# A diffusion step: other queues for the u and y transfers, and GELU in fused operations with its second half behind the first splits of the GLU

## The chip, the cores and the metric

The kernel runs on one core of one Trainium2 chip. The metric is the device time of an execution, in microseconds. Three runs of the kernel before took 2743.68, 2744.83 and 2745.60 us, so the median is 2744.83.

## The reference, cut to what matters

One layer runs over 640 tokens, 128 of context and 512 latent ones, of width 2048. An adaLN-modulated, normalised input goes through one projection into `u_a`, `v_a` and `u_b`, of 1024 columns each. A chunk mixer takes the first two, a bidirectional state-space mixer the third; both are normalised and projected by `w_out`; a squared-ReLU MLP follows. The change lies in the state-space mixer:

```
u = x.reshape(bsz, seq_len, N_SSM_GROUPS, SSM_GROUP)          # 64 groups of 16
h_f = ssm_scan(u, lam_f, bb_f, h0_f, False)
h_b = ssm_scan(u, lam_b, bb_b, h0_b, True)
y = (einsum("ghp,blgp->blgh", c_f, h_f) + einsum("ghp,blgp->blgh", c_b, h_b)).real
y = y.reshape(bsz, seq_len, D_SSM) + d_skip * x
y = gelu(y)                                                   # tanh form
y = y * sigmoid(y @ w_glu + b_glu)
```

All is float32. Large products are made of three products of float32r halves, so each weight chunk is split into a high part (`wh`, ScalarE) and a low part (`wl`, VectorE), and so is each activation.

## The kernel before, in words

**Layout.** Tokens stand in 80 blocks of L=8 and one empty column, NJ=81 in all. The projection gives `u` with channels on partitions; the scan wants (time in block, channel of group) on partitions. So `u` goes through DRAM (`ud`): for each of 8 channel blocks `cb` a tile `us` is filled by VectorE (L324) and stored by 8 DMAs, one for each time in the block (L327). Odd ones are issued by ScalarE, even ones by GpSimd. Each moves 128 rows of 81 floats. The tile `us` has two buffers.

**The slots.** From L442 on the instructions of each engine are kept in the order in which the code issues them (`P`, `Kept`; the profile gives all of them one line, L451, so they are told apart by tiles). Work is cut into slots (`slot`, L496). A slot asks for the raw weights of chunk c+2 on SP (`raw_of`), makes the high part of chunk c+1 on ScalarE (`hi_of`) and the low part on VectorE (`lo_of`), and multiplies chunk c on TensorE. Other work is put into a slot by `at(t, phase, f)`: `sp`, `evac`, `act`, `dve`, `pe`, `end` in that order, and `mid0` and `mid1` within an `as` chunk.

**The stretch of the change.** Slots 33 to 48 multiply the chunk mixer's half by `w_out` (tiles `as`, 30 matmuls of 512 columns a slot). When the scan is done, which is at slot e = 42 here, `s5_rest` spreads 16 pieces `s5_out(u)` over the slots from e on, three a slot. Each makes 12 small products into a PSUM tile `yp` (two buffers), and ScalarE copies it over the input tile `U`. After u = 7 (slot 44) half 0 of y is complete, after u = 15 (slot 47) half 1. `y_store(half)` writes a half to DRAM (`yd`) with 8 DMAs, four on SP and four on ScalarE, each 16 partitions by 32 rows of 81 floats. `yc_load(k)` reads 128 channels back, blocks 0 to 3 from half 0 and 4 to 7 from half 1, and waits for all stores of its half. `gelu(k)` computes tanh-GELU into `yb`. `yb_split(k)` makes the two halves of `yb` that the GLU multiplies. The first two GLU chunks (`glu_pair`) take two column blocks: the first chunk needs blocks k = 0 to 3, the second k = 4 to 7.

**Before**, half 0 is stored in slot 45 and loaded in 46 and 47; gelu 0 and 1 stand in slot 47, 2 and 3 in 48; half 1 is stored at the end of 47, loaded in 48, and gelu 4 to 7 stand at the end of 48. Slot 49 splits blocks 0 to 3, multiplies the first GLU chunk, and splits 4 to 7.

[...]

Of the kernel before, what the change touches and what calls it, by code (L numbers as in the profile page):

```python
# [12 lines left out]
F32 = mybir.dt.float32  # L13
# [3 lines left out]
AF = mybir.ActivationFunctionType  # L17
OP = mybir.AluOpType
# [5 lines left out]
NT = 640  # L24
# [3 lines left out]
GH = 16  # L28
NS = 64
L = 8  # L30
NJ = 81
# [12 lines left out]
def build(nc, tc, a, out, tap=None):  # L44
    tap = tap or {}
    V = nc.vector
    S = nc.scalar
    G = nc.gpsimd
# [8 lines left out]
    def a20(shape, dt, name):  # L57
        return fr.tile(shape, dt, name=name, tag="a20", bufs=4)
# [4 lines left out]
    def pm(name="pm"):  # L63
        return pp.tile([128, 512], F32, name=name, tag="pm", bufs=4)
# [16 lines left out]
    def dram(name, shape):  # L81
        return dr.tile(shape, F32, name=name)
# [4 lines left out]
    yd = dram("yd", [DC, L, NJ])  # L87
# [79 lines left out]
    def load_w(src, n1, n2, prio=WPRIO):  # L167

        with tc.high_priority(offset=prio):
            raw = wtile("r", [128, n1, n2], F32)  # L170
            nc.sync.dma_start(raw, src)
            hi = wtile("h", [128, n1, n2], F32R)
            lo = wtile("l", [128, n1, n2], F32R)
            S.activation(hi, raw, AF.Copy)
            V.tensor_sub(lo, raw, hi.bitcast(F32))
        return hi, lo
# [5 lines left out]
    def ws_mm(ps, hi, lo, k, kk, c, ah, al, first, last, tr):  # L182
        for i, (st, mv) in enumerate(((hi, ah), (hi, al), (lo, ah))):
            for p, (t0, n) in zip(ps, tr):
                T.matmul(p[:, :n], st[:, kk, c:c + 128], mv(k)[:, t0:t0 + n],  # L185
                         start=(first and i == 0), stop=(last and i == 2))
# [39 lines left out]
    for tb in range(NTB):  # L226
        if tb:
            for n in range(2):
                p = pm("pos")
# [70 lines left out]
    def u_chunk(kc0, nk):  # L300
        kb = slice(kc0, kc0 + nk)
        cpl = 8 // nk
        for cb in range(8):
            if cb % cpl == 0:
                whi, wlo = load_w(w_in[:, kb, 2 * DC + cb * 128:2 * DC + (cb + cpl) * 128], nk, cpl * 128, 0)
            ps = [pm("ub"), pm("ub")]
            for k in range(kc0, kc0 + nk):
                ws_mm(ps, whi, wlo, k, k - kc0, (cb % cpl) * 128, ah, al, k == kc0, k == kc0 + nk - 1, FULL)
            if kc0 + nk == NK and cb == 6:
                ahead.append(load_w(w_in[:, 0:8, DC:DC + 128], 8, 128, 0))  # L310
            if kc0 + nk < NK:
                for p_, (t0, n) in zip(ps, FULL):
                    dst = uacc[:, cb, t0:t0 + n]
                    if kc0 == 0:
                        S.activation(dst, p_[:, :n], AF.Copy)
                    else:
                        V.tensor_add(dst, dst, p_[:, :n])
            else:
                us = main.tile([128, L, NJ], F32, name="us", tag="t25", bufs=2)
                V.memset(us[:, :, 16:17], 0.0)  # L320
                jt = lambda t: t.rearrange("p (j t) -> p t j", t=L)
                for i, t0, n, j0 in ((0, 0, 128, 0), (0, 128, 192, 17), (1, 320, 320, 41)):
                    o = t0 - i * 320
                    V.tensor_tensor(us[:, :, j0:j0 + n // L], jt(uacc[:, cb, t0:t0 + n]), jt(ps[i][:, o:o + n]), op=OP.add)  # L324

                for t in range(L):
                    (nc.scalar if t % 2 else nc.gpsimd).dma_start(  # L327
                        bass.AP(tensor=ud.tensor, offset=ud.offset + ((7 - t) * GH * NG + cb * 8) * NJ,
                                ap=[[NJ, 8], [NG * NJ, GH], [1, NJ]]), us[:, t, :])

    for i in range(len(CH) + 1):
        if i < len(CH):
            h_chunk(*CH[i])
        if i:
            u_chunk(*CH[i - 1])
# [44 lines left out]
    q, w = vt_[3], vt_[4]  # L380
# [19 lines left out]
    for lo_, n in ((1, 1), (2, 2), (4, 4)):  # L400
        for d in range(2):
# [8 lines left out]
            t2 = p0.tile([128, 4, NG], F32, name="pt", tag="acs", bufs=2)  # L410
# [42 lines left out]
    V, S, T, G, SY = [Kept(e) for e in (nc.vector, nc.scalar, nc.tensor, nc.gpsimd, nc.sync)]  # L453
# [5 lines left out]
    def at(t, phase, f):  # L459
        assert t >= now[0], (t, now[0], phase)  # L460
        todo.setdefault((t, phase), []).append(f)
# [334 lines left out]
    HG = 32  # L796
    JS = NJ + 1
    Us, pbs = [], {}
    ydv = yd.rearrange("(g c) t j -> t c g j", c=GH)
# [140 lines left out]
    for h in range(8):  # L940
        t = t0_ + 2 * h
# [74 lines left out]
    def s5_out(uu):  # L1016
        t_, o_ = so_.pop(uu)
        half, u = divmod(uu, 8)
        U = Us[half]
        p = px("yp")  # L1020
        for g in range(4):
            gg = u * 4 + g
            gx = half * HG + gg
            o = p[:, g * NJ:(g + 1) * NJ]
            T.matmul(o, t_[:, g, :], U[:, gg, :], start=True, stop=False)
            T.matmul(o, o_[:, 0, g, :], X[:, 0, gx, 0:NJ], start=False, stop=False)
            T.matmul(o, o_[:, 1, g, :], X[:, 1, gx, 1:1 + NJ], start=False, stop=True)
        S.activation(U[:, u * 4:u * 4 + 4, :], p[:, 0:4 * NJ].rearrange("p (g j) -> p g j", j=NJ), AF.Copy)
        so_load(uu + 3)

    def y_store(half):
        for tq in range(8):
            (SY if tq % 2 else S).dma_start(ydv[tq][:, half * HG:(half + 1) * HG, :], Us[half][tq * GH:(tq + 1) * GH])

    K0 = float(np.sqrt(2.0 / np.pi))
    yb, ycs = [None, None], {}
    ybs = []

    def yb_part(k, lo):
        return ybs[lo][:, k, :]  # L1040

    ybk = lambda k: yb[k // 4][:, k % 4, :]

    def yc_load(k):
        if k < 4:
            ycs[k] = main.tile([128, L, NJ], F32, name="yc", tag="t25", bufs=2)
        else:
            if k % 2 == 0:
                ykeep.append(pbs["pb"].tile([128, 1536], F32, name="yk", tag="so", bufs=3))
            ycs[k] = ykeep[-1][:, k % 2 * 768:k % 2 * 768 + L * NJ].rearrange("p (t j) -> p t j", t=L)  # L1050
        SY.dma_start(ycs[k], yd[k * 128:(k + 1) * 128])

    def gelu(k):
        yc = ycs.pop(k)
        if k % 4 == 0:
            yb[k // 4] = pbs["uy"].tile([128, 4, NT], F32, name="yb", tag="uy", bufs=2)
        w1 = pbs["pb"].tile([128, L, NJ], F32, name="w1", tag=("ya", "vc")[k % 2], bufs=1)
        S.activation(w1, yc, AF.Square)
        V.tensor_scalar(w1, w1, 0.044715, 1.0, op0=OP.mult, op1=OP.add)
        V.tensor_mul(w1, w1, yc)  # L1060
        S.activation(w1, w1, AF.Tanh, scale=K0)
        V.tensor_scalar(w1, w1, 1.0, 0.5, op0=OP.add, op1=OP.mult)
        for c0, c1, j0 in ((0, 128, 0), (128, 640, 17)):
            nj = (c1 - c0) // L
            V.tensor_tensor(ybk(k)[:, c0:c1].rearrange("p (j t) -> p t j", t=L), w1[:, :, j0:j0 + nj],
                            yc[:, :, j0:j0 + nj], op=OP.mult)

    def yb_split(k):
        if k == 0:
            ybs.extend(a20([128, 8, NT], F32R, f"yb{i}") for i in range(2))  # L1070
        S.activation(yb_part(k, 0), ybk(k), AF.Copy)
        V.tensor_sub(yb_part(k, 1), ybk(k), yb_part(k, 0).bitcast(F32))
# [41 lines left out]
    def s5_rest(e):  # L1114

        where = [(e + u // 3, (("mid0", "mid1", "pe") if e + u // 3 < 49 else ("pe",) * 3)[u % 3]) for u in range(16)]
        for u, w in enumerate(where):
            at(*w, lambda u=u: s5_out(u))
        t, t2 = where[7][0], where[15][0]
        at(t + 1, "sp", lambda: y_store(0))  # L1120
        for k in range(4):
            at(t + 2 + k // 2, "sp", lambda k=k: yc_load(k))
            at(t + 3 + k // 2, "act", lambda k=k: gelu(k))
        at(t2, "end", lambda: y_store(1))
        for k in range(4, 8):
            at(t2 + 1, "sp", lambda k=k: yc_load(k))
            at(t2 + 1, "end", lambda k=k: gelu(k))
        return t + 5, t2 + 1

    flow[0] = iter(())  # L1130
    e = None
    t = 16
    while t < 49 or e is None or t < max(g0, g1):
# [4 lines left out]
        if scanned and e is None and t >= 38:  # L1138
            e = t
            g0, g1 = s5_rest(e)  # L1140
# [14 lines left out]
    g1 = max(g1, g0)  # L1155
    for k in range(4):
        at(g0, "act", lambda k=k: yb_split(k))
        at(g1, "end", lambda k=4 + k: yb_split(k))
    t = g0
    while cur[0] < len(chunks):  # L1160
        c = cur[0] - 48
# [18 lines left out]
    V, S, T, G = nc.vector, nc.scalar, nc.tensor, nc.gpsimd  # L1180
# [146 lines left out]
    half = lambda w: w.rearrange("(j t p) c -> t p j c", t=2, p=128)  # L1327
# [347 lines left out]
    p = ps["2"].tile([128, 512], F32, name="trms", tag="zp", bufs=2)  # L1675
# [83 lines left out]
```

## Time and profile before

| | |
|---|---|
| median of three runs | 2744.83 us |
| profiled execution | 2745.85 us |
| its span | 2744.0 us, 43078 instructions |
| TensorE (PE) | 2608.5 us busy, 95% |
| VectorE (DVE) | 1939.3 us, 71% |
| ScalarE (ACT) | 1116.6 us, 41% |
| GpSimd (POOL) | 85.3 us, 3% |
| DMA | 519.37 MB, mean 189 GB/s |

PE is TensorE's matmuls, PEld its weight loads, SPq and ACTq the instructions with which SP and ScalarE issue DMAs; those of GpSimd stand under POOL. Busy time of TensorE is 95% of the span, so the other engines' shares say little by themselves. What matters is the few places where TensorE stands still, and which instruction ended that.

### The profile page before, as it was taken

What the parts mean: (1) busy time and instruction counts of PE and PEld (TensorE: products, weight loads), DVE (VectorE), ACT (ScalarE), POOL (GpSimd) and SP (SyncE); (2) the same over time, 40 slices, a digit from 0 to 9 for tenths busy, and PEclk for the clock granted to TensorE, in tenths of its full rate; (3) what the DMA queues carried; (4) which work ended last, traced back from release to release, by engine and by line L of the source; (5) the groups of instructions that cost most, each with busy time, mean ns of one, the idle gap of its engine ahead of it and who ended that gap; (6) DMA issues with size and microseconds to landing.
All of it is one profiled execution on the core that took longest, in us unless ns stands there. A gap on an engine that the chain in (4) does not pass through costs nothing.

```text
span 2744.0 us, 43078 instructions
## 1 busy us (share of the span) xinstructions
PE 2608.5 (95%) x17217; PEld 2410.7 (88%) x17217; DVE 1939.3 (71%) x2870; ACT 1116.6 (41%) x1806; POOL 85.3 (3%) x105
## 2 busy tenths in 40 slices
PE   8997999989959988899999999998999999999997
PEld 5687888877848665899999999998999999999996
DVE  4565997888055356777777777776677777777786
ACT  4121432222134255655555555554433232323253
POOL 0003221000001000000000000000000000000000
PEclk9998999999979998899999999999999999999998
DMA  9846766454746796355665556557466356446553
GB/s 302 293 165 158 213 199 204 143 182 151 202 103 222 253 334 204 89 177 176 186 183 173 178 174 188 181 176 267 132 219 219 114 196 219 158 148 227 179 174 112
DMA packets 459434, 519.37 MB, mean 189 GB/s; under 512 B 31409, under 2 KB 375633, under 8 KB 451809
## 3 DMA queue, kind: packets, MB, share of 16 engines
q1 hardware_dynamic: 440240, 507.84, 56.9%
q10 hardware_dynamic: 17456, 7.43, 1.1%
q8 instruction: 136, 2.23, 0.3%
q0 software_dynamic: 1536, 1.35, 0.2%
q14 instruction: 66, 0.53, 0.1%
HBM read 410.08 MB, written 106.45 MB: 188 GB/s over the span
## 4 chain that ended last, share of the span: by engine, by line
PE 82%; DMA 6%; DVE 6%; ACT 3%; issue 2%; SPq 1%; POOL 0%; ACTq 0%; DVEq 0%; POOLq 0%
PE X L1381 32%; PE Y L1381 16%; PE Z L1381 8%; PE ws L451 7%; PE ub L185 4%; PE ob L1284 3%; PE as L451 3%; PE ada L195 2%; DMA vc<-vd 2%; PE adaq L451 1%; PE yp L451 1%; DMA x2d<-wx 1%; DMA wr<-in_w_out_dram 1%; PE adaq L195 1%; PE x1p L451 1%
## 5 line engine op out<-in xcount | busy, mean ns | idle before, releaser
L1368 ACT ACTIVATE wh<-wx 128x1024 fp32r<-128x1024 f32 x223 | 235.8, 1058 | 310.1 <-PE X L1381 140.8
L1373 DVE TENSOR_TENSOR wl<-wx,wh 128x1024 fp32r<-128x1024 f32 x223 | 272.8, 1223 | 73.9 <-ACT wh L1368 71.9
L1381 PE MATMUL X<-B,wh 128*128 128x320 f32 x1376 | 308.0, 312 | 3.3 <-ACT wx L1368 3.3
L1381 PEld LDWEIGHTS X<-B,wh 128*128 128x128 f32 x1376 | 233.7, 191 | 3.6 <-ACT wx L1368 3.6
L1381 PE MATMUL X<-B,wl 128*128 128x320 f32 x688 | 214.2, 311 | 0.0
L1381 PE MATMUL X<-B,wx 128*128 128x320 f32 x1008 | 154.6, 309 | 0.0
L1381 PE MATMUL Y<-B,wh 128*128 128x320 f32 x672 | 150.6, 312 | 3.5 <-ACT wh L1368 3.5
L1381 PEld LDWEIGHTS X<-B,wx 128*128 128x128 f32 x1008 | 149.5, 188 | 0.0
L1456 DVE TENSOR_TENSOR wx<-wx 128x320 fp32r<-128x320 f32 x192 | 93.0, 485 | 78.2 <-ACT wx L1453 78.2
L1579 DVE TENSOR_TENSOR facc<-facc,X 128x640 f32<-128x640 f32 x116 | 95.1, 820 | 73.1 <-PE X L1381 72.4
L451 ACT ACTIVATE wh<-wr 128x1024 fp32r<-128x1024 f32 x55 | 58.3, 1060 | 207.7 <-DMA wr<-in_w_in_dram 82.1
L1381 PE MATMUL X<-B2n,wh 128*128 128x320 f32 x608 | 134.7, 309 | 0.0
L1381 PEld LDWEIGHTS X<-B,wl 128*128 128x128 f32 x688 | 131.0, 190 | 0.0
L451 DVE TENSOR_TENSOR wl<-wr,wh 128x1024 fp32r<-128x1024 f32 x55 | 68.5, 1246 | 84.9 <-ACT wh L451 84.3
L1368 ACT ACTIVATE wh<-wr 128x1024 fp32r<-128x1024 f32 x76 | 80.4, 1058 | 107.5 <-PE X L1381 51.3
L451 PE MATMUL ws<-hTh,wh 128*128 128x320 f32 x512 | 122.6, 321 | 0.4 <-DVE us L324 0.4
L451 PE MATMUL ws<-hTh,wl 128*128 128x320 f32 x512 | 118.9, 314 | 3.6 <-DVE wl L451 3.6
L1368 ACT ACTIVATE wx<-wr 128x1024 fp32r<-128x1024 f32 x75 | 79.4, 1058 | 104.7 <-PE X L1381 53.3
L1368 ACT ACTIVATE wx<-wx 128x1024 fp32r<-128x1024 f32 x74 | 78.3, 1058 | 103.5 <-PE X L1381 48.7
L451 PE MATMUL ws<-hTl,wh 128*128 128x320 f32 x512 | 118.7, 313 | 0.0
L1381 PEld LDWEIGHTS Y<-B,wh 128*128 128x128 f32 x672 | 113.9, 190 | 3.8 <-ACT wh L1368 3.8
L1373 DVE TENSOR_TENSOR wx<-wr,wx 128x1024 fp32r<-128x1024 f32 x75 | 91.8, 1224 | 28.0 <-ACT wx L1368 27.3
(380 smaller groups left out, 6685.5 us busy)
## 6 DMA issues: line engine op xcount, KB each, us to landing
wx<-in_w_ff_dram SPq DMA_DIRECT2D x169, 512.0 KB
x2d<-wx SPq DMA_DIRECT2D x224, 320.0 KB
wr<-in_w_ff_dram SPq DMA_DIRECT2D x87, 512.0 KB
aw<-in_w_ada_dram SPq DMA_DIRECT2D x80, 512.0 KB
was<-in_w_ada_dram SPq DMA_DIRECT2D x64, 512.0 KB
B2n<-x2d SPq DMA_DIRECT2D x24, 1280.0 KB
wr<-in_w_in_dram SPq DMA_DIRECT2D x48, 512.0 KB
wr<-in_w_out_dram SPq DMA_DIRECT2D x48, 512.0 KB
```

The lines of the kernel that those rows point to most:

```text
L185: T.matmul(p[:, :n], st[:, kk, c:c + 128], mv(k)[:, t0:t0 + n], start=(first and i == 0), stop=(last and i == 2))
L195: T.matmul(p[32 * j:32 * j + 32], sc[:, 2 * (k0 + i):2 * (k0 + i) + 32], w[:, i, :], start=k0 + i < 4, stop=k0 + i >= NK - 4)
L451: return lambda *p, **k: P(f(*p, **k))
L1284: T.matmul(p, st[:, k0 + kk, tsl], mv[:, kk, :], start=(k0 + kk == 0 and i == 0), stop=(k0 + kk == 7 and i == 2))
L1368: P(S.activation(hls[n][0], raw, AF.Copy))
L1373: P(V.tensor_sub(lo, raw, hi.bitcast(F32)))
L1381: P(T.matmul(p, st[:, j, c:c + 128], xv(j, x), start=first and j == 0 and i == 0, stop=j == nj - 1 and i == 2, skip_group_check=not first))
L1456: P(V.tensor_sub(hlt[i][:, 1], raw, hlt[i][:, 0].bitcast(F32)))
L1579: P(V.tensor_add(dst, dst, src))
```

## The change

The odd u stores go from ScalarE's queue to SP's. All y stores and loads go to GpSimd's queue, each store right behind the last copy of its half, and the loads behind the stores. GELU takes two blocks at a time: the factor 0.044715 goes into the square's scale, one VectorE operation makes (1 + .)y, ScalarE halves y by a copy, and one operation with a sum in it makes the result. Blocks 0 and 1 stand at the end of slot 45, 2 and 3 at the end of 46; GELU of blocks 4 to 7 stands at the end of slot 49, behind the splits of 0 to 3 and the first GLU chunk, with the splits of each pair right behind the pair.

```
--- before.py
+++ after.py
@@ -324,7 +324,7 @@
                     V.tensor_tensor(us[:, :, j0:j0 + n // L], jt(uacc[:, cb, t0:t0 + n]), jt(ps[i][:, o:o + n]), op=OP.add)
 
                 for t in range(L):
-                    (nc.scalar if t % 2 else nc.gpsimd).dma_start(
+                    (nc.sync if t % 2 else nc.gpsimd).dma_start(
                         bass.AP(tensor=ud.tensor, offset=ud.offset + ((7 - t) * GH * NG + cb * 8) * NJ,
                                 ap=[[NJ, 8], [NG * NJ, GH], [1, NJ]]), us[:, t, :])
 
@@ -1030,7 +1030,7 @@
 
     def y_store(half):
         for tq in range(8):
-            (SY if tq % 2 else S).dma_start(ydv[tq][:, half * HG:(half + 1) * HG, :], Us[half][tq * GH:(tq + 1) * GH])
+            G.dma_start(ydv[tq][:, half * HG:(half + 1) * HG, :], Us[half][tq * GH:(tq + 1) * GH])
 
     K0 = float(np.sqrt(2.0 / np.pi))
     yb, ycs = [None, None], {}
@@ -1048,22 +1048,27 @@
             if k % 2 == 0:
                 ykeep.append(pbs["pb"].tile([128, 1536], F32, name="yk", tag="so", bufs=3))
             ycs[k] = ykeep[-1][:, k % 2 * 768:k % 2 * 768 + L * NJ].rearrange("p (t j) -> p t j", t=L)
-        SY.dma_start(ycs[k], yd[k * 128:(k + 1) * 128])
-
-    def gelu(k):
-        yc = ycs.pop(k)
-        if k % 4 == 0:
-            yb[k // 4] = pbs["uy"].tile([128, 4, NT], F32, name="yb", tag="uy", bufs=2)
-        w1 = pbs["pb"].tile([128, L, NJ], F32, name="w1", tag=("ya", "vc")[k % 2], bufs=1)
-        S.activation(w1, yc, AF.Square)
-        V.tensor_scalar(w1, w1, 0.044715, 1.0, op0=OP.mult, op1=OP.add)
-        V.tensor_mul(w1, w1, yc)
-        S.activation(w1, w1, AF.Tanh, scale=K0)
-        V.tensor_scalar(w1, w1, 1.0, 0.5, op0=OP.add, op1=OP.mult)
-        for c0, c1, j0 in ((0, 128, 0), (128, 640, 17)):
-            nj = (c1 - c0) // L
-            V.tensor_tensor(ybk(k)[:, c0:c1].rearrange("p (j t) -> p t j", t=L), w1[:, :, j0:j0 + nj],
-                            yc[:, :, j0:j0 + nj], op=OP.mult)
+        G.dma_start(ycs[k], yd[k * 128:(k + 1) * 128])
+
+    def gelu(*ks):
+
+        ws, ys = [], [ycs.pop(k) for k in ks]
+        for k in ks:
+            if k % 4 == 0:
+                yb[k // 4] = pbs["uy"].tile([128, 4, NT], F32, name="yb", tag="uy", bufs=2)
+            ws.append(pbs["pb"].tile([128, L, NJ], F32, name="w1", tag=("ya", "vc")[k % 2], bufs=1))
+        for w1, yc in zip(ws, ys):
+            S.activation(w1, yc, AF.Square, scale=float(np.sqrt(0.044715)))
+        for w1, yc in zip(ws, ys):
+            V.scalar_tensor_tensor(w1, w1, 1.0, yc, op0=OP.add, op1=OP.mult)
+        for w1, yc in zip(ws, ys):
+            S.activation(w1, w1, AF.Tanh, scale=K0)
+            S.activation(yc, yc, AF.Copy, scale=0.5)
+        for k, w1, yc in zip(ks, ws, ys):
+            for c0, c1, j0 in ((0, 128, 0), (128, 640, 17)):
+                nj = (c1 - c0) // L
+                V.scalar_tensor_tensor(ybk(k)[:, c0:c1].rearrange("p (j t) -> p t j", t=L), w1[:, :, j0:j0 + nj], 1.0,
+                                       yc[:, :, j0:j0 + nj], op0=OP.add, op1=OP.mult)
 
     def yb_split(k):
         if k == 0:
@@ -1117,15 +1122,13 @@
         for u, w in enumerate(where):
             at(*w, lambda u=u: s5_out(u))
         t, t2 = where[7][0], where[15][0]
-        at(t + 1, "sp", lambda: y_store(0))
-        for k in range(4):
-            at(t + 2 + k // 2, "sp", lambda k=k: yc_load(k))
-            at(t + 3 + k // 2, "act", lambda k=k: gelu(k))
-        at(t2, "end", lambda: y_store(1))
-        for k in range(4, 8):
-            at(t2 + 1, "sp", lambda k=k: yc_load(k))
-            at(t2 + 1, "end", lambda k=k: gelu(k))
-        return t + 5, t2 + 1
+        for half, w in ((0, where[7]), (1, where[15])):
+            at(*w, lambda half=half: y_store(half))
+            for k in range(4 * half, 4 * half + 4 - 2 * (half == 0)):
+                at(*w, lambda k=k: yc_load(k))
+        at(t + 1, "end", lambda: (gelu(0, 1), yc_load(2), yc_load(3)))
+        at(t + 2, "end", lambda: gelu(2, 3))
+        return t + 3, t2 + 1
 
     flow[0] = iter(())
     e = None
@@ -1155,7 +1158,7 @@
     g1 = max(g1, g0)
     for k in range(4):
         at(g0, "act", lambda k=k: yb_split(k))
-        at(g1, "end", lambda k=4 + k: yb_split(k))
+    at(g1, "end", lambda: (gelu(4, 5), yb_split(4), yb_split(5), gelu(6, 7), yb_split(6), yb_split(7)))
     t = g0
     while cur[0] < len(chunks):
         c = cur[0] - 48
```

On SP, at the end of the u stage (`wr` are raw weights, `bc` tables of the scan), the order of the two kernels, + being new:

```order
 L296 DMA xd<-big 128x1024 x4
 L171 DMA wr<-in_w_in_dram 128x4x256 x2
+L327 DMA ud<-us 8x16x81 x8
 L171 DMA wr<-in_w_in_dram 128x8x128
+L327 DMA ud<-us 8x16x81 x24
 L451 DMA bc<-in_bc_dram 128x512
```

Thirty-two u stores now stand on SP ahead of the scan's first tables and of the weights and `aw` loads behind these.

On GpSimd, between the last sum of squares of the chunk mixer (`diag`) and the first of the GLU (`sqb`); `yk` are the loaded blocks 4 to 7:

```order
 L451 TENSOR_TENSOR ks<-ks 128x16
 L451 TENSOR_TENSOR diag<-diag,sq 128x640 x8
+L451 DMA yd<-U 16x32x81 x8
+L451 DMA yc<-yd 128x648 x4
+L451 DMA yd<-U 16x32x81 x8
+L451 DMA yk<-yd 128x648 x4
 L451 TENSOR_TENSOR sqb<-sqb,sq 128x640 x7
```

GpSimd had nothing to do there; now all sixteen stores and eight loads stand in its one queue.

On ScalarE, at the border of slots 45 and 46 (`U<-yp` is the copy of an `s5_out`, `so` are its loaded tables, `w` the GELU's work tiles):

```order
 L451 ACTIVATE U<-yp 128x324
 L451 DMA so<-kd 128x1x128 x4
+L451 ACTIVATE w_7161<-yc 128x648
+L451 ACTIVATE w_7162<-yc 128x648
+L451 ACT_TABLE_LOAD
+L451 ACTIVATE w_7161<-w_7161 128x648
+L451 ACTIVATE yc<-yc 128x648
+L451 ACTIVATE w_7162<-w_7162 128x648
+L451 ACTIVATE yc<-yc 128x648
 L451 ACTIVATE wh<-wr 128x1024
 L451 ACTIVATE U<-yp 128x324
 L451 DMA so<-kd 128x1x128 x4
```

The first GELU pair stands ahead of slot 46's weight split and of its three copies of `yp`; it stood in slot 47.

## Rows read from the trace of the kernel before

**Rows 1.** The page, the chain that ended last: share of the span by engine.

```profile
PE 82%; DMA 6%; DVE 6%; ACT 3%; issue 2%; SPq 1%; POOL 0%; ACTq 0%; DVEq 0%; POOLq 0%
```

**Rows 2.** Waits of TensorE, 725 to 830 us: total, times, longest.

```profile
PE ws L451 <- ACT yb L451: 27.9, 1, 27.9
```

**Rows 3.** The chain in order of time, 600 to 900 us: start us, us, what.

```profile
719.88 2.82 PE as L451 x12
...
726.77 2.66 PE yp L451 x24
...
743.42 4.36 PE yp L451 x24
...
811.54 9.14 PE ws L451 x46
821.67 7.26 PE ws L451 x48
```

**Rows 4.** Windows: busy us (count) of PE, PEld, DVE, ACT, POOL; PEclk, DMA share, GB/s.

```profile
744.00:748.00 4.00, 4.00 (x22) 3.99 (x22) 0.30 (x1) 0.40 (x1) 0.00 (x0) 0.58 0.75 171
```

**Rows 5.** Timeline of ACT, 684 to 835 us: start, us, operation, [idle before <-releaser].

```profile
725.38 0.44 ACT L451 ACTIVATE U<-yp 128x324 f32<-128x324 f32 x1 [5.02 <-PE yp L451]
...
734.86 7.07 ACTq L451 DMA_DIRECT2D yd<-U  x4
741.98 1.06 ACT L451 ACTIVATE wh<-wr 128x1024 fp32r<-128x1024 f32 x1 [10.71 <-DMA yd<-U]
...
766.56 1.28 ACT L451 ACT_TABLE_LOAD   x1
...
772.53 0.42 ACT L451 ACTIVATE U<-yp 128x324 f32<-128x324 f32 x1
...
801.16 0.73 ACT L451 ACTIVATE w<-yk 128x648 f32<-128x648 f32 x1
...
805.00 0.73 ACT L451 ACTIVATE w<-yk 128x648 f32<-128x648 f32 x1
...
809.79 5.11 ACT L451 ACTIVATE yb<-yb 128x640 fp32r<-128x640 f32 x8
```

**Rows 6.** Timeline of SP, same stretch.

```profile
729.86 4.96 SPq L451 DMA_DIRECT2D yd<-U  x4
...
790.12 1.76 SPq L451 DMA_DIRECT2D yk<-yd  x4
```

**Rows 7.** Timeline of DVE, same stretch.

```profile
801.82 1.31 DVE L451 TENSOR_TENSOR yb<-w,yk 128x128 f32<-128x128 f32 x2
...
803.49 0.83 DVE L451 TENSOR_TENSOR w<-w,yk 128x648 f32<-128x648 f32 x1
```

**Rows 8.** Timeline of POOL, 198 to 262 us.

```profile
210.26 1.97 POOL L327 DMA_DIRECT2D ud<-us  x3 [209.81 <-DVE us L324]
213.12 0.61 POOL L327 DMA_DIRECT2D ud<-us  x1 [0.89 <-issue]
215.60 1.23 POOL L327 DMA_DIRECT2D ud<-us  x2 [1.88 <-issue]
...
252.37 0.59 POOL L327 DMA_DIRECT2D ud<-us  x1 [1.03 <-issue]
```

**Rows 9.** The tile ud: time to landing, of GpSimd's u stores.

```profile
DMA to landing us min/median/max: 2.0/3.7/6.5
```

**Rows 10.** DMA queues, 205 to 262 us: packets, MB, share of 16 engines.

```profile
q0 software_dynamic: 1536, 1.35, 10.3%
```

**Rows 11.** Timeline of DVE, 198 to 262 us.

```profile
219.78 0.38 DVE L324 TENSOR_TENSOR us<-uacc,ub 128x128 f32<-128x128 f32 x1 [7.27 <-DMA ud<-us]
```

**Rows 12.** Timeline of SP, 198 to 262 us.

```profile
238.71 0.37 SPq L451 DMA_DIRECT2D wr<-in_w_in_dram  x1
...
250.02 1.40 SPq L451 DMA_DIRECT2D aw<-in_w_ada_dram  x3
```

**Rows 13.** Timeline of PE, 225 to 260 us.

```profile
255.51 3.40 PE L451 MATMUL adaq<-aw,sc 128*32 128x512 f32 x8 [9.62 <-DMA aw<-in_w_ada_dram]
```

## The prediction

> **What bounds the kernel now.** I read the page first: the chain that ended last is TensorE for most of the span [rows 1], so an edit counts only where TensorE stands still. The change touches two such places.
>
> The larger is between the last `w_out` chunk and the GLU. TensorE's waits from 725 to 830 us name it: 27.9 us in one piece, for ScalarE's `yb` [rows 2]. The lists of ScalarE, SP and VectorE say what fills it. The last `s5_out` result (U of u=15) is copied at 772.53 and done at 772.95 [rows 5]; half 1 of y is then stored, SP issues the four `yk` loads at 790.12 [rows 6], and GELU 4 to 7 runs one block each 3.84 us (805.00 less 801.16) [rows 5]. Only then come the splits of `yb`, at 809.79, for blocks 0 to 3 too. The GLU's first two chunks are the first two ws entries of the chain; the second ends at 821.67 + 7.26 = 828.93 [rows 3]. [...]
>
> The second place is the end of the u stage, where TensorE idles 9.62 us for an `aw` load [rows 13].
>
> **The change part by part.** *GELU in fused operations.* VectorE loses two scalings a block and ScalarE gains one copy. A pair costs ScalarE six operations of about 0.7 us [rows 5] and VectorE two of 0.83 and two write-outs of 1.31 [rows 7]. Laid out in the new order, from the landing of the first load of half 1: squares to 1.4, tanh and copy of block 4 to 2.8, of block 5 to 4.2; write-outs to 4.2 and 5.6; split of block 5 to 6.3; the same again for 6 and 7, whose last low half is done at about 13.6. The GLU's second chunk then has its second column block left, half of 7.26. That is 17.2 us from landing to the end of that chunk.
>
> *Second half behind the first splits.* Splits 0 to 3 and the first GLU chunk now run while half 1 travels. That takes 7.3 us of TensorE work out of the wait.
>
> *y through GpSimd's queue.* Here lies the price, and the trace does not show it: GpSimd stored only u before. Its u stores begin with three back to back (210.26), then a gap of 0.89, then one of 1.88 [rows 8], with nothing for it to wait on but the queue. One u store lands 3.7 us after its issue by the median, 2.0 to 6.5 [rows 9]: the fourth starts 2.86 us after the first, the next 2.5 later. I read this as a limit on work in flight: three of 128 rows of 324 bytes (16 x 8 rows of 81 floats, L327). A y store has 512 such rows (16 x 32, L1033), so I take it that one y store is in flight at a time. Its bytes are four times as many: 32 u stores took 10.3% of 57 us of all DMA engines [rows 10], 0.18 us each, so a y store takes 0.73, or 0.55 more. One store: 3.7 + 0.55 = 4.25 us; eight: 34 us. Low end: the two hardware queues' own pace for eight, from 729.86 to 741.93, 12.1 us [rows 5, 6]. High end: the pace of u's GpSimd half, which is as many rows (32 x 128 = 8 x 512) from 210.26 to 252.96, 42.7 us [rows 8]. So a store costs 1.5 to 5.3 us; I take 4.25, the one worked out from single transfers, and use it for a load as well.
>
> [...]
>
> *Sum at the GLU.* U of u=7 is copied by 725.38 + 0.44 = 725.8 [rows 5]. Eight stores: 759.8; the first load, which waits for all eight: Y = 764.05. GELU(0,1) now stands in ScalarE's order right behind slot 45 and holds up the next weight split and the copies of slot 46. TensorE gets there on its own: slot 45 starts at 726.77 + 2.66 = 729.4 [rows 3], a slot is 2.5 x 2.82 + 3 x 2.66 = 15.0, and the third `yp` of slot 46, which needs a copied bank, is due 12.4 later, at 756.8. ScalarE is through two squares, a table load of 1.28, four more, a split of 1.06 and a copy of 0.44 at Y + 7.0 = 771.05 [rows 5]. So TensorE stands 14 us. Then one `yp`, 12 `as` and one `yp` are 8.1 us, plus 3 at the lower clock, by the row after the stall of 742 [rows 3, 4]: the copy of u=15 ends near Y + 18 = 782.05, 9.1 later than before. Eight stores and a load: 820.3. Then 17.2 and some 1.5 for the lower clock after a second idle stretch: 839.0, against 828.93. That is +10.1 us. In formula, with p for a store: the chunk ends at 762.5 + 18p, and breaks even at p = 3.69. Behind it the two programs agree.
>
> *u stores on SP.* us waits for landings of u stores (7.27 us at 219.78) [rows 11], and GpSimd's half stays and sets that pace; ScalarE's half was never the later one for long. SP's order now puts all 32 ahead of bc, wr and aw. Before, wr went at 238.71 and aw at 250.02 [rows 12]. After, four stores of the last block and these loads (1.25 MB) follow each other from about 246 to 250. Worst: aw, whose 512 KB reached TensorE 5.5 us after their issue [rows 12, 13], queues behind two and a half times as many bytes: I allow 5 us for these and 1.5 for issue, +6.5. Best: the stage without bc and wr in it frees us 2 to 3 us sooner: -3. I take 0, since the later issue and the earlier end are alike in size.
>
> Total: the profiled execution, 2745.85 (span 2744.0 and 1.85 around it), + 10.1 = 2756; the median of the runs lies 1.0 below the profiled one, so 2755.
>
> **The rivals.** *Stores overlap.* If GpSimd's stores run like those of the hardware queues (1.5 us each), Y is 742, before slot 45 ends at 744.4; nothing stalls, u=15 is copied at 765.6, half 1 has landed at 781.8 and the chunk ends at 799: -30, or 2715. For it: the DMA engines need only 0.73 us a store. Against: three u stores and then gaps.
>
> *One at a time, but short.* With the quickest landing, 2.0 + 0.55 = 2.55 a store, Y is 748.8 and the stall goes (755.8 against 756.8); u=15 is copied at 765.4 and the chunk ends at 807: -22, or 2723. Every p below 3.69 is a gain, and the median landing of rows 9 with nothing added for size is just there. Against: the y stores of half 0 share the DMA engines with 512 KB loads.
>
> *u stage late.* If aw lands after bc, wr and the stores, +6.5 on the forecast: 2761. For it: one queue in order. Against: SP has nothing else to do there.
>
> **How the numbers follow.** A change under 0.2%, 5.5 us, can't be told from none. One at a time near 4.25 us, the forecast: 0.52, of which 0.44 is slower and 0.08 (p from 3.4 to 4.0) is no change; its own range is 2742 to 2774, the latter from p = 5.3. One at a time and short: 0.23, of which 0.15 is faster and 0.08 no change. Overlapping: 0.17, faster. u stage late: 0.08, of which 0.06 is slower and 0.02 no change. Together faster 0.32, no change 0.18, slower 0.50. The range leaves out the overlapping stores and a little above: 2728 to 2774.
>
> **What would show it.** GpSimd's y stores a landing apart, near 4 us, with yc behind the eighth; TensorE idle in the slot after the first GELU pair; a second idle stretch between the GLU's two first chunks, in place of the 27.9 us. Wrong, if two y stores start within 2 us of each other, or if eight take less than 29 us; wrong on u, if the `adaq` group starts over 4 us from 255.51.

## The result, and the profile after

The changed kernel takes 2766.57 us (median of four runs, 2766.21 to 2766.83) against 2744.26 for the kernel before (four runs): 22.3 us more, a ratio of 1.0083, 95% interval 1.0065 to 1.0100. A second measurement, beside other runs of the kernel before, gave 1.0078 (1.0063 to 1.0092). The forecast was 2755, slower, in a range of 2728 to 2774. The direction came out as forecast, and so did the stores one at a time and the two idle stretches; the loss is twice the size.

The profiled execution of after took 2766.21 us, its span is 2764.1. The page's chain that ended last, shares by engine:

```profile
PE 79%; DMA 6%; DVE 6%; issue 5%; ACT 2%; POOL 1%; SPq 1%; DVEq 0%; ACTq 0%; POOLq 0%
```

Against [rows 1] TensorE lost three points and "issue" gained three: time in which the chain stands on an engine that waits for nothing the trace shows. That engine is GpSimd. TensorE's waits, 690 to 870 us (total, times, longest):

```profile
PE ws L451 <- ACT yb L451: 27.9, 3, 23.4
PE yp L451 <- ACT U L451: 19.7, 1, 19.7
PE ws L451 <- DVE yb L451: 0.9, 2, 0.6
```

The 27.9 us of [rows 2] are not gone: the same total is now in three pieces, of which one is 23.4, and 19.7 us for a copy of `yp` have come on top. The timeline of GpSimd (POOL) shows why (start, us, operation, count, idle before):

```profile
726.08 0.68 POOL L451 DMA_DIRECT2D yd<-U  x1 [107.14 <-ACT U L451]
731.10 0.64 POOL L451 DMA_DIRECT2D yd<-U  x1 [4.34 <-issue]
737.31 0.64 POOL L451 DMA_DIRECT2D yd<-U  x1 [5.57 <-issue]
...
761.65 0.63 POOL L451 DMA_DIRECT2D yd<-U  x1 [3.64 <-issue]
766.14 1.14 POOL L451 DMA_DIRECT2D yc<-yd  x2 [3.86 <-DMA yd<-U]
...
789.72 0.65 POOL L451 DMA_DIRECT2D yd<-U  x1 [12.16 <-ACT U L451]
794.64 0.66 POOL L451 DMA_DIRECT2D yd<-U  x1 [4.27 <-issue]
...
822.70 0.64 POOL L451 DMA_DIRECT2D yd<-U  x1 [6.10 <-issue]
827.23 2.23 POOL L451 DMA_DIRECT2D yk<-yd  x4 [3.89 <-DMA yd<-U]
```

An issue takes 0.64 us, and then GpSimd stands 3.4 to 6.1 us although its next instruction depends on nothing: the stores go one by one. From the first store of half 0 to its loads it is 766.14 - 726.08 = 40.1 us, of half 1 827.23 - 789.72 = 37.5, that is 5.0 and 4.7 us a store. The loads, four in a row within 2.23 us, are not held up like this. In the trace's list of DMA issues, 690 to 830 us, the y stores have a median time to landing of 4.2 us (last column):

```profile
yd<-U POOLq DMA_DIRECT2D x16, 162.0 KB, 4.2
```

What ScalarE does with it, in its timeline:

```profile
725.19 0.44 ACT L451 ACTIVATE U<-yp 128x324 f32<-128x324 f32 x1 [5.02 <-PE yp L451]
...
744.27 0.44 ACT L451 ACTIVATE U<-yp 128x324 f32<-128x324 f32 x1 [3.62 <-PE yp L451]
...
769.36 0.74 ACT L451 ACTIVATE w<-yc 128x648 f32<-128x648 f32 x1 [24.65 <-DMA yc<-yd]
...
788.87 0.44 ACT L451 ACTIVATE U<-yp 128x324 f32<-128x324 f32 x1 [1.55 <-PE yp L451]
...
801.60 2.60 ACT L451 ACTIVATE yb<-yb 128x640 fp32r<-128x640 f32 x4
830.55 1.54 ACT L451 ACTIVATE w<-yk 128x648 f32<-128x648 f32 x2 [26.35 <-DMA yk<-yd]
```

The copy of u=7 comes at the same time as in [rows 5] (725.19 against 725.38), so nothing of the loss lies ahead of it in this trace. Then ScalarE waits 24.65 us for the first load, and the next copy of a `yp`, which stands behind the GELU pair in ScalarE's order, starts only at 775.84, 31.57 us after the one at 744.27. The splits of blocks 0 to 3 (801.60) do run before half 1 is there, as the change has it, 8.2 us earlier than the 809.79 of [rows 5]; but GELU 4 to 7 starts only at 830.55.

The chain in order of time (start, us, what):

```profile
761.65 3.71 DMA yd<-U
...
776.32 5.41 PE yp L451 x24
781.73 4.47 PE as L451 x12
...
843.35 6.73 PE ws L451 x34
850.08 1.00 PE adaq L451 x8
```

The GLU's second chunk ends at 850.08, where in [rows 3] it ended at 828.93: 21.15 later, of 20.1 us of difference in the spans. So the stage holds the whole loss, and what lies behind the chunk takes no longer than before. `yp` takes 5.41 us behind the stall, twice its 2.66 of [rows 3]. The window of the stall in after has the granted clock as the third number from its end:

```profile
760.00:780.00 20.00, 3.68 (x17) 3.69 (x18) 5.31 (x7) 7.01 (x10) 2.85 (x5) 0.53 0.39 90
```

0.53 of full speed, in a window in which TensorE was busy for 3.68 us, all of it at the end. Cut into pieces of 4 us, the clock is 0.50 from 764 to 784 us, and 1.00 from 788 to 792; [rows 4] had 0.58.

### The profile page after: what moved, and what is told of

Read it like the earlier page. It is cut to its first block, busy times and chain, and to the rows that moved or that the text cites. A ratio compares the mean times of both kernels' runs of the same rounds, so it can differ in the third digit from the quotient of the medians.

```text
span 2764.1 us, 43100 instructions
## 1 busy us (share of the span) xinstructions
PE 2607.9 (94%) x17217; PEld 2409.5 (87%) x17217; DVE 1932.9 (70%) x2854; ACT 1122.4 (41%) x1814; POOL 99.7 (4%) x129
## 3 DMA queue, kind: packets, MB, share of 16 engines
q8 instruction: 136, 2.23, 0.3%
## 4 chain that ended last, share of the span: by engine, by line
PE 79%; DMA 6%; DVE 6%; issue 5%; ACT 2%; POOL 1%; SPq 1%; DVEq 0%; ACTq 0%; POOLq 0%
PE X L1384 32%; PE Y L1384 16%; PE Z L1384 8%; PE ws L451 5%; PE ub L185 4%; PE ob L1287 4%; PE as L451 3%; PE ada L195 2%; DMA vc<-vd 1%; DMA awr<-in_w_ada_dram 1%; PE yp L451 1%; PE adaq L451 1%; PE tp L250 1%; PE adaq L195 1%; DMA wr<-in_w_ff_dram 1%
## 5 line engine op out<-in xcount | busy, mean ns | idle before, releaser
L1376 DVE TENSOR_TENSOR wx<-wr,wx 128x1024 fp32r<-128x1024 f32 x75 | 91.8, 1224 | 27.9 <-ACT wx L1371 27.1
```

The source lines that it names most:

```text
L1376: P(V.tensor_sub(lo, raw, hi.bitcast(F32)))
```

## The experiments

There are eleven runs, in three sittings on three chips (e1 to e4, e5 to e8, e9 to e11), each beside the kernel before on the same chip; e10 repeats after, and e11 repeats e4. In the table, "stage" is the time from ScalarE's start on the copy of u=7 to the end of the GLU's second chunk in the profiled execution; the last column is the difference of the medians. The stage of before is 828.93 - 725.38 = 103.55 us [rows 3, 5].

| | u stores | y stores | stage, us | stage less before | median less before |
|---|---|---|---|---|---|
| after | SP | GpSimd | 124.9 | +21.3 | +22.3 |
| e8 (before, y alone) | ScalarE | GpSimd | 129.5 | +26.0 | +24.8 |
| e4 | ScalarE | GpSimd | 122.9 | +19.4 | +19.5 |
| e10 (after again) | SP | GpSimd | 125.3 | +21.8 | +21.2 |
| e11 (e4 again) | ScalarE | GpSimd | 127.0 | +23.4 | +18.3 |
| e1 (1280 bytes) | SP | GpSimd | 102.3 | -1.3 | +0.8 |
| e2 (half rows) | SP | GpSimd | 99.6 | -3.9 | -0.8 |
| e3 | SP | SP, ScalarE | 100.4 | -3.2 | -1.6 |
| e5 (half rows, 1280) | ScalarE | GpSimd | 92.8 | -10.8 | -12.4 |
| e6 | ScalarE | SP | 92.2 | -11.4 | -14.7 |
| e9 (half rows, 1280) | ScalarE | GpSimd, SP | 79.1 | -24.5 | -24.8 |
| e7 (before, u alone) | SP | SP, ScalarE | 103.9 | +0.4 | +2.2 |

The last two columns go together within 3.3 us in every row but e11, where they are 5.1 apart: most of the time is decided in this one stage. The stage of one kernel varies too (e4 and e11, 122.9 and 127.0), and single executions differ elsewhere (the profiled span of e5 is 19.2 us below that of before, with a stage 10.8 shorter), so differences of a few microseconds in this column show nothing by themselves.

**Is it the number in the build?** `dynamic_dma_scratch_size` is 1024 in the build of before (L1745) and of after. Theory R takes it for room, in bytes, that GpSimd's stores share and that holds one y store; what stands in these bytes no run shows. The rivals in the expectations, G and C, put the price elsewhere than in that room, so that e1 would be as slow as after; by C it goes with the number of stores, so that e2 would be far slower.

e1, this number alone:

```
-    nc = bacc.Bacc("TRN2", ..., dynamic_dma_scratch_size=1024)
+    nc = bacc.Bacc("TRN2", ..., dynamic_dma_scratch_size=1280)
```

> The changed kernel with 1280 in place of 1024 bytes set aside for GpSimd's descriptors, nothing else. Theory R (room for descriptors): a y store starts only when the one before has landed and given its room back; with a quarter more room two fit, so the stores of a half start about 2.5 us apart in the mean in place of 4.7 to 5.0, TensorE's stall in slot 46 goes, and the time falls by 30 to 40 us, to 2726 to 2736. Rival G (GpSimd itself needs 4 to 5 us for the 512 rows of a store, whatever the room) and rival C (one transfer at a time by rule): starts stay 4.7 to 5.0 us apart, 2766.

Measured: 2743.21 us, ratio 1.0002 (0.9990 to 1.0015): the +22.3 of after are down to +0.8. GpSimd's timeline in e1:

```profile
719.96 1.31 POOL L451 DMA_DIRECT2D yd<-U  x2 [105.17 <-ACT U L451]
725.39 0.64 POOL L451 DMA_DIRECT2D yd<-U  x1 [4.12 <-issue]
...
750.20 1.22 POOL L451 DMA_DIRECT2D yc<-yd  x2 [6.48 <-DMA so<-kd]
...
773.12 1.31 POOL L451 DMA_DIRECT2D yd<-U  x2 [11.59 <-ACT U L451]
...
795.26 2.34 POOL L451 DMA_DIRECT2D yk<-yd  x4 [3.86 <-PE adaq L451]
```

Two stores start in a row (x2 in 1.31 us), in both halves; they take 30.2 and 22.1 us in place of 40.1 and 37.5. Nothing but a number in the build was changed, and the queue and the count of stores are those of after, so G falls. The time is above the 2726 to 2736 expected: half 0 gained 9.9 us, half 1 15.4. Why half 0 gained less is not shown. There is a gap of 6.97 us in it, and from 728.5 to 732 us, inside this gap, the DMA engines' mean busy share was 90% or more, with weight and table loads among the rest; that these held the stores up was not tested.

e2, the number back at 1024, each store cut in two:

```
-            G.dma_start(ydv[tq][:, half * HG:(half + 1) * HG, :], Us[half][tq * GH:(tq + 1) * GH])
+            for q in range(2):
+                G.dma_start(ydv[tq][:, half * HG + 16 * q:half * HG + 16 * q + 16, :], Us[half][tq * GH:(tq + 1) * GH, 16 * q:16 * q + 16])
```

> The changed kernel with each y store cut in two of 256 rows, so 16 stores a half, the room left at 1024 bytes. Theory R: three of these fit, as three u stores did, so a half takes 16 x 1.3 to 1.6 = 21 to 26 us in place of 37.5 to 40; 2726 to 2738. Rival G (time goes with rows): a half takes as long as now, 2766. Rival C (one transfer at a time): 16 x 4.3 = 69 us a half, and the time rises by 60 us or so, to 2825.

Measured: 2741.69 us, ratio 0.9991 (0.9981 to 1.0001). GpSimd's timeline in e2:

```profile
721.70 1.69 POOL L451 DMA_DIRECT2D yd<-U  x3 [19.85 <-ACT U L451]
...
752.36 1.29 POOL L451 DMA_DIRECT2D yc<-yd  x2 [3.10 <-DMA yd<-U]
...
775.23 1.75 POOL L451 DMA_DIRECT2D yd<-U  x3 [10.72 <-ACT U L451]
...
796.22 1.13 POOL L451 DMA_DIRECT2D yk<-yd  x2 [1.78 <-PE ws L451]
```

The time is above the 2726 to 2738 expected. Behind one store of each half, which needs only the first four u and went earlier, the other fifteen took 30.7 us in half 0 and 21.0 in half 1, where 21 to 26 were expected for a half. But twice as many stores for the same bytes, and the +22.3 of after become -0.8: C falls, and three stores of 256 rows start in a row where there was one of 512. So the y stores start by ones in after, by twos in e1 and by threes in e2 (x1, x2 and x3 above). The u stores, of 128 rows, start in the numbers of those of 256: three in a row with 1024 bytes, in [rows 8] and likewise in after, e3, e4 and e7 (1.96 to 2.00 us), and four with 1280, as here in e1:

```profile
211.73 2.58 POOL L327 DMA_DIRECT2D ud<-us  x4 [211.28 <-DVE us L324]
```

**The other queues.** e3, y stores by turns on SP and ScalarE as before, loads on SP, GELU in its new place:

```
-            G.dma_start(ydv[tq]...
+            (SY if tq % 2 else S).dma_start(ydv[tq]...
-        G.dma_start(ycs[k], yd[k * 128:(k + 1) * 128])
+        SY.dma_start(ycs[k], yd[k * 128:(k + 1) * 128])
```

> The changed kernel with its y stores back on SP and ScalarE by turns and its y loads on SP; the fused GELU, its places and the u stores on SP stay. If the queue is what costs, the stores of a half take some 12 us as before the change, GELU(0,1) no longer holds ScalarE, and the time is 2715 to 2728, some 5 us of it for ScalarE's queue held by four stores in slot 44. Rival: the new places of GELU or the u stores cost something themselves; then it stays above 2745.

Measured: 2740.89 us, ratio 0.9990 (0.9981 to 0.9998). The stores were quick, and the expected gain did not come. SP's timeline in e3:

```profile
777.66 5.08 SPq L451 DMA_DIRECT2D yd<-U  x4
792.51 1.76 SPq L451 DMA_DIRECT2D yk<-yd  x4
794.32 0.98 SPq L451 DMA_DIRECT2D wr<-in_w_glu_dram  x2
```

and ScalarE's:

```profile
801.41 1.06 ACT L451 ACTIVATE wh<-wr 128x1024 fp32r<-128x1024 f32 x1 [12.29 <-DMA wr<-in_w_glu_dram]
```

The `yk` loads wait on SP for all stores of their half, 9.8 us behind the last issue (777.66 + 5.08 to 792.51), and the GLU's weights wait behind them in the same queue, although they need none of it. Their split stands on ScalarE ahead of the splits of blocks 0 to 3, and so TensorE waits 14.8 us in one piece before the GLU. TensorE's waits in e3:

```profile
PE ws L451 <- ACT yb L451: 16.6, 2, 14.8
PE as L451 <- ACT acc L451: 9.1, 1, 9.1
```

The second is the price of ScalarE's four stores of half 0: they hold its queue for 6.90 us, and TensorE waits 9.1 us for the sums (`acc`) behind them, where some 5 were allowed. The wait was not taken away but moved. So e6: all y stores on SP, the loads left on GpSimd, where no load of weights stands behind them.

e5 is e2 with 1280 bytes, e6 as just said, both with the odd u stores back on ScalarE.

> After with each y store cut in two of 256 rows, 1280 bytes set aside for GpSimd's descriptors in place of 1024, and the odd u stores back on ScalarE. [...]

> After with all y stores on SP's queue, the loads left on GpSimd's, and the odd u stores back on ScalarE: the loads that wait for the stores stand ahead of nothing else. Theory R: eight stores at SP's pace of 1.24 us take 10 us, y of half 0 is back at 741, no stall at yp, U of u=15 copied near 766, half 1 back near 781, the GLU's second chunk ends at 798 to 806 against 828.9; 2713 to 2724 us against 2742. Theory B (won in front of the GLU, given back behind it): the chunk ends as early, 2735 to 2743.

Measured: e5 2730.03, ratio 0.9955 (0.9940 to 0.9970); e6 2727.73, ratio 0.9951 (0.9936 to 0.9965). Of e5 2718 to 2730 us were expected, with four stores in flight, 16 to 21 us for the 16 of a half and the GLU's second chunk done at 804 to 812. Both are faster than before, by less than expected: the GLU's second chunk ends 92.8 and 92.2 us after the start of the copy of u=7, where 79 to 87 and 73 to 81 follow from the times expected. GpSimd's timeline in e5:

```profile
718.09 2.23 POOL L451 DMA_DIRECT2D yd<-U  x4 [19.85 <-ACT U L451]
...
742.26 1.22 POOL L451 DMA_DIRECT2D yc<-yd  x2 [5.33 <-DMA so<-kd]
...
767.90 2.31 POOL L451 DMA_DIRECT2D yd<-U  x4 [10.95 <-ACT U L451]
...
787.26 1.13 POOL L451 DMA_DIRECT2D yk<-yd  x2 [2.71 <-DMA yd<-U]
```

Four in a row now, where e2 had three with 1024. That it would be four was the author's estimate; what room a store takes no run shows. Half 0 still takes 24.2 us from there and half 1 19.4: what sets the pace with four in flight no run tells apart. TensorE's waits in e5:

```profile
PE ws L451 <- ACT yb L451: 10.7, 3, 6.1
PE yp L451 <- ACT U L451: 6.4, 1, 6.4
```

and in e6:

```profile
PE ws L451 <- ACT yb L451: 12.3, 2, 9.5
PE yp L451 <- DMA so<-od: 3.2, 1, 3.2
```

In e6 the price has moved again: SP's timeline has the eight stores of half 0 from 726.57 on for 12.16 us, and a table load (`so`) behind them that a `yp` group then waits for. That is the 3.2 us. The longer piece, 9.5 us, begins on SP as well:

```profile
774.73 8.58 SPq L451 DMA_DIRECT2D yd<-U  x8
783.41 2.22 SPq L451 DMA_DIRECT2D wr<-in_w_glu_dram  x2
```

The GLU's weights stand behind the eight stores of half 1. By the chain they land 9.45 us after their issue at 783.41, and their split on ScalarE holds up those of blocks 0 to 3, as in e3. So with the loads off SP this wait fell from 14.8 to 9.5 us, and what is left of it runs through the stores themselves. Theory B, that a gain here is given back later, is against the table: the stage's gain and the median's agree, 10.8 with 12.4 and 11.4 with 14.7.

e9 follows from both: the first store of each pair needs only the first four u of its half, so those go early on GpSimd, and the second ones on SP. Its edit against e5:

```
-                G.dma_start(ydv[tq][:, half * HG + 16 * q...
+                (SY if q else G).dma_start(ydv[tq][:, half * HG + 16 * q...
```

> The version with y stores of 256 rows, 1280 bytes for descriptors and the u stores on ScalarE, with the second store of each pair on SP instead of GpSimd. GpSimd's eight need only the first four u of a half, so they go before the half is complete; eight of 81 KB on SP are left. Theory: what is late is the way of a half's y from its last copy to GELU, so halving what is left of it gains: copy of u=7 to the end of the GLU's second chunk 78 to 86 us, against 92.8 with all on GpSimd, 2716 to 2724 us. Rival: SP's hold on the loads behind the stores costs what it did with all stores on SP: 90 to 93 us, 2726 to 2731.

Measured: 2720.05 us against 2744.81, ratio 0.9907 (0.9892 to 0.9923), the fastest version, with a stage of 79.1 us as expected: 24.8 us less than before and 46 less than after by the second measurement. GpSimd's timeline in e9:

```profile
705.20 2.29 POOL L451 DMA_DIRECT2D yd<-U  x4 [86.68 <-ACT U L451]
...
718.68 1.19 POOL L451 DMA_DIRECT2D yc<-yd  x2 [5.59 <-DMA so<-od]
...
756.77 2.29 POOL L451 DMA_DIRECT2D yd<-U  x4
```

GpSimd's eight stores of half 0 are out before the copy of u=7, at 724.80 in this run; SP's eight follow it. The loads of blocks 0 and 1 (718.68) go out before that copy too. A store of 16 of the 32 groups of a half holds channels 0 to 255 of it, which are its first two blocks, so these loads wait for the first store of each pair alone, and GELU(0,1) no longer waits for half 0 as a whole. The expectation did not count that; how much of the gain comes from it, and how much from the fewer stores left at the end, no run tells apart. TensorE's waits in e9:

```profile
PE ws L451 <- ACT yb L451: 6.8, 2, 3.6
PE as L451 <- ACT acc L451: 1.5, 1, 1.5
```

The stall at `yp` is gone, and 6.8 of the 27.9 us are left.

**The queue without the new GELU.** e8 is the kernel before with the y stores and loads on GpSimd, and nothing else:

```
-            (SY if tq % 2 else S).dma_start(ydv[tq]...
+            G.dma_start(ydv[tq]...
-        SY.dma_start(ycs[k], yd[k * 128:(k + 1) * 128])
+        G.dma_start(ycs[k], yd[k * 128:(k + 1) * 128])
```

> Before with only the y stores and loads moved to GpSimd's queue; GELU, its place and the u stores as before. Queue's price by the measured 5.0 and 4.7 us a store: half 0 back at 770, gelu 0 in slot 47 holds up the copies of U, u=15 copied near 783, half 1 back at 826, then the old GELU order's 36 us to the end of the GLU's second chunk: 862 against 828.9, +33, 2775 us against 2742; so the fused GELU and its new place would be worth some 12 us of after. Rival: the new GELU order is worth nothing, then this is as slow as after, 2762 to 2766.

Measured: 2767.25 us, ratio 1.0095 (1.0079 to 1.0111), +24.8 where +33 was expected; that is nearer the rival's 2762 to 2766. TensorE's waits in e8:

```profile
PE ws L451 <- ACT yb L451: 46.4, 1, 46.4
PE as L451 <- DVE wl L451: 11.5, 1, 11.5
```

The size was off mostly in one place: I had GELU 0, in slot 47, delay the copy of u=15 by 10 us against before. It came 52.8 us after the copy of u=7, against 47.2 in [rows 5]. What follows stands in part: the queue alone costs as much as the whole change or a little more. What the new GELU and its place win back with it is e8 less e4, 5.3 us by the medians, or 6.5 with e11 for e4; but they ran on different chips, and the intervals overlap (from 1.0079 in e8, up to 1.0081 in e4 and 1.0090 in e11), so the size of this gain is not shown. With quicker stores (e6) the same GELU is part of a version 14.7 us below before.

**The u stores.** Three comparisons. e4 and e11 are after with them back on ScalarE, e10 is after beside e11, e7 is before with them on SP:

```
-                    (nc.sync if t % 2 else nc.gpsimd).dma_start(
+                    (nc.scalar if t % 2 else nc.gpsimd).dma_start(
```

> The changed kernel with the odd u stores back on ScalarE. By the traces the adaq group after the u stage started at about the same time counted from the stage's start, so 2764 to 2769, no change within 0.2%. Rival (u stage late): the u stores on SP cost up to 6 us, 2760.

> Before with only the odd u stores moved to SP. The prediction's value: no difference (bounds -3 to +6.5). From the run of after with them back on ScalarE, 4.6 us less than after: +3 to +5, with GpSimd's first u store some 1.5 us later and the adaq wait near 10.6 us. Measured in five rounds: 2740 to 2744 by the one, 2745 to 2748 by the other, against 2742 for before.

> The changed kernel again, beside the next one on one chip, to weigh the u stores alone. By the first measurement 1.0083 of before, 2763 to 2767 us.

> The changed kernel with the odd u stores back on ScalarE, again. If the u stores on SP cost nothing, the same as the kernel beside it within 2 us; if they cost what the two earlier comparisons leaned to, 2 to 5 us less.

Measured: e4 2762.00 (ratio 1.0068, 1.0056 to 1.0081); e7 2744.65 (1.0008, 0.9998 to 1.0018); e10 2766.05 and e11 2763.15 (1.0078 and 1.0076, intervals of 0.0014 to each side). e4 lies between its forecast and its rival's, e7 between its two forecasts, and e10 and e11 in theirs. The runs are more spread here than the first four of after, which lay within 0.6 us: e7's go from 2740.79 to 2749.73. By the medians all three comparisons lean to a cost on SP, of 4.6 (against the first measurement of after), 2.2 and 2.9 us; by the ratios e10 and e11 differ by 0.0002, which is 0.5 us. Neither of the two made side by side is clear of nothing. TensorE's wait for `aw`, 195 to 270 us, in after:

```profile
PE adaq L451 <- DMA aw<-in_w_ada_dram: 10.6, 1, 10.6
```

against 9.62 in [rows 13], and 10.8 in e10 against 9.8 in e11. But in e7, with the stores on SP, it is 9.3, where 10.6 was expected. Over all runs with 1024 bytes the wait is 8.7 to 10.8 us with these stores on SP and 8.9 to 9.8 with them on ScalarE, and from GpSimd's first u store to the `adaq` group it is 44.8 to 46.6 and 44.8 to 46.2 us. So the stage itself shows no clear cost; whether there is one elsewhere stays open.

## Why the prediction was right about the sign and short on the size

**One store at a time: right, by a count that does not hold.** After has x1, and there are x2, x3 and x4 where the number in the build or the size was changed, so a bound on work in flight is there. But the prediction read it in rows: three u stores of 128, 384 in all. By that a y store of 512 rows would be as much as the four u stores that did not start together, and yet e2 had three of 256 rows, 768 in all, in the same 1024 bytes. In the traces a u store of 128 rows counts as much as a y store of 256: three of either start together with 1024 bytes ([rows 8], e2), four with 1280 (e1, e5). Why the two are alike no run shows; the argument by rows does not have it, and that it led to one at a time as well was luck.

**The price of a store: the step that failed.** The sum put 3.7 + 0.55 = 4.25 us for a store, "worked out from single transfers". The landing itself was well met, 4.2 us by the median. But a time to landing is not the step from one store to the next. The last store of half 0 lands at 761.65 + 3.71 = 765.36, by the chain, and the next instruction begins at 766.14, 0.78 later. And eight in a row cost eight means, while I added up medians: the steps go from 4.0 to 6.7 us, their median is 4.56, their mean (40.06 + 37.51) / 16 = 4.85. Sixteen times the missing 0.60 is 9.6 us, most of the 11.1 by which the chunk ended later than forecast (850.1 less 839.0). The upper bound, 42.7 / 8 = 5.3 from u's own pace, was a little nearer (some 0.5 off), though with three stores in flight there and one here that may be chance.

**The formula.** It took a load as a store: 762.5 + 18p. With the measured steps, 5.0 and 4.7, it gives 762.5 + 9 x 5.0 + 9 x 4.7 = 849.8, against 850.08. Within it errors cancel: a load took 3.2 us (766.14 to 769.36), 1.6 less than a store, twice; the stall's tail, from Y to the end of the copy of u=15, took 789.31 - 769.36 = 19.95 in place of 18, and the last GELU to the chunk's end 19.5 in place of 18.7.

**The stall behind the first GELU pair: right in kind.** TensorE stood for a copy of `yp`, 19.7 us where 14 were forecast. Y was 5.3 us late (769.36 against 764.05), and that is nearly all of the difference.

**The new order of GELU: right, and worth little on this queue.** The splits of blocks 0 to 3 and the first GLU chunk run before half 1 is there. But the chunk of TensorE work put into the wait is short against a half that comes 41 us after its last copy (789.31 to 830.55).

**The lower clock.** 3 us were put in after the first stall, by the `yp` group of [rows 3] that took 4.36 us in place of 2.66, in a stretch with a granted clock of 0.58 [rows 4]. In after, with the clock at 0.50 from 776 to 784 us, `yp` lost 5.41 - 2.66 = 2.75 and `as` 4.47 - 2.82 = 1.65 us in the chain, 4.4 in all. Some 1.5 were put in behind the second idle stretch; there the clock was 0.67 from 844 to 848 us and 1.00 from 848 on.

**u stores on SP: 0 in the sum, not refuted.** `adaq` waited 1.0 us longer in after, but not in e7 (9.3 us). It started at 257.7 in after, 2.2 behind [rows 13], under the 4 us named as wrong; GpSimd's first u store was 1.5 us late already, so no more than 0.7 us of it is the queue's.

**The rivals.** Overlapping stores did not come of themselves, but e1, e2 and e5 made them, and the time against before went from +22.3 to +0.8, -0.8 and -12.4. The break-even was placed too high, though: with 3.8 and 2.8 us a store (e1, 30.2 and 22.1 for eight) the formula's 18p is 59.4 and the chunk ends 7 us earlier than before, where the stage of e1 gained 1.3. The short store (2.55 us) fell with the measured 4.85. The late u stage, +6.5, is more than any of the three comparisons gives.

## What to carry to other kernels

When stores go to GpSimd's queue, count how many can be in flight: look for gaps marked "issue" between instructions that depend on nothing (3.4 to 6.1 us in after), and see what a store of another size (e2), or another `dynamic_dma_scratch_size` (e1), does to them. For a chain of transfers one at a time, take the mean step from start to start of a chain that exists, not the median time to landing of single ones. And a load that waits for stores belongs in a queue in which nothing that could run stands behind it (14.8 us of TensorE in e3); the stores hold up what stands behind them too (9.5 us in e6).

## What the runs showed that I had not expected

A `dynamic_dma_scratch_size` of 1280 in place of 1024 is worth some 21 us here (+22.3 to +0.8): two stores in flight in place of one took half 1 from 37.5 to 22.1 us.

Twice as many GpSimd stores of half the size were quicker than whole ones, -0.8 against +22.3 us, although each issue still costs 0.56 us of GpSimd in place of 0.64.

On SP the same eight stores took 12.16 us in e6 for half 0 and 8.58 for half 1; eight of half the size took 8.58 and 4.22 in e9. SP's pace for these rows is not one number, and the loads that stand behind the stores pay for it (the 3.2 and 9.5 us of e6).
